# Layer 1's mixer gate summed by VectorE, block 0's products of chunk 1 in the passage, and a new list for the mixer

## The chip, the cores and the metric

One Trainium2 chip, one NeuronCore of it. The metric is the device time of one execution in microseconds (us). The engines are TensorE (PE in the profile; its weight loads are PEld), VectorE (DVE), ScalarE (ACT), GpSimd (POOL) and SyncE (SP), which issues all the loads of weights.

## The reference

Two layers work on x (256 tokens, 1024 features, f32) under a condition c (1024 values). Each has a mixer and an FFN:

```python
mod = silu(c) @ w_ada[l] + b_ada[l]
sh1, sc1, gt1, sh2, sc2, gt2 = split(mod, 6)
h = rms_norm(x, g_pre_mix) * (1 + sc1) + sh1
q, k, v, pz = split(h @ w_in[l])            # 4 x 512 columns
ao = causal_attention(rope(q), rope(k), v)  # 8 heads of 64
po = multiscale_pool(pz, w_pool, pool_scale)
y = concat(rms_norm(ao), rms_norm(po)) @ w_out[l]
x = x + gt1 * rms_norm(y, g_post_mix)
h = rms_norm(x, g_pre_ffn) * (1 + sc2) + sh2
u = causal_conv3(h @ w_up[l]) + conv_b      # 2 x 2816 columns
x = x + gt2 * rms_norm((silu(u_a) * u_g) @ w_down[l], g_post_ffn)
```

With 256 tokens there is one attention block, so the attention is plain causal softmax attention. gt1 is what this text calls the mixer gate.

## The kernel before

**Products in three parts.** Every f32 operand of a large product is split in two: a rounded part (hi for weights, hh for activations, sh for the FFN's gated activations) and the rest (lo, hl, sl). `mm3` does hi,hh, then lo,hh, then hi,hl, 512 columns each. ScalarE casts the hi, VectorE subtracts for the lo.

**The stream of weights.** `Stream` lists all weights as units of up to 128x2048 f32 in the order in which they are wanted. SyncE loads them in that order into four raw buffers (`RAW_BUFS`); a unit's load is issued when the unit four places ahead in the list is done with. `high` and `low` turn half units into parts (hi and lo, `PART_BUFS` = 8 of each); `ahead` makes parts up to six ahead of their use.

**Tokens and features.** Tokens stand in two blocks of 128. `Normed.trans` transposes the normed x (xn) on TensorE into tiles T, 128 features (a chunk, k or j from 0 to 7) by 256 tokens, and `Normed.make` scales and shifts a chunk into hh (ScalarE) and h, then hl (VectorE).

**Stages.** Layer 0's mixer; its FFN, 22 steps of an up product (u), the convolution and gate (`conv_glu`) and the down product (d), the last six down products kept to the end (`DEFER`); then the passage: the down products end for block 0 and block 1 (`tail`), two norms per block (ry for the FFN's output, rx for the new x), then layer 1's qkv stage, which goes over eight chunks and for each over two blocks; layer 1's mixer; layer 1's FFN.

**The modulation.** Most of mod comes from VectorE: `dot` multiplies a 128x1024 half unit with silu(c) on all partitions and sums each row (CUSTOM_DVE_ANT_0 in the trace, ISA in the instruction order), one column of 128 outputs at a time; scale, shift and the last gate come so. The mixer gate comes from TensorE: `ada_gt` multiplies silu(c) with 1 MB units of w_gt, in plain f32, into the bank gacc; ScalarE copies it (grow), `group_trans` transposes it (gT) and `group_cols` adds it up.

**What sets the order.** In the mixers an order written out by hand: `ORDER[l]` is a list of steps, and `hold` (or `held`) keeps the engines to the order in which the program states the instructions. Names: `ph` a quarter of the pz product of a block, `cq`, `ck`, `cK`, `cv`, `cz`, `cZ` copies out of PSUM, `ro` the rotary of a block, `kq` the transposes of q or k, `sc` scores, `mx`, `ex`, `rc`, `nm` softmax, `yP` and `wo` out products, `hi` and `lo` weight parts, `xu`, `xN`, `tr` the new x, its norm and its transposes, `wm` n dummy transposes. Everywhere else a scheduler orders each engine's instructions.

## Time and profile before

| | |
|---|---|
| three runs | 600.38, 602.14, 603.25 us; median 602.14 |
| the profiled execution | 601.36 us, of which 599.6 us from the first to the last instruction |
| mean granted TensorE clock | 0.998 |
| TensorE busy | 585.6 us |
| VectorE busy | 499.4 us |

Times in the rows count from the first instruction. TensorE's busy time counts a product from its issue to its modelled end, and products overlap, so what one costs is read from the distance of two starts. Idle time stands in brackets with the instruction that ended it.

### The profile page before, as it was taken

What the parts mean: (1) busy time and instruction counts of PE and PEld (TensorE: products, weight loads), DVE (VectorE), ACT (ScalarE), POOL (GpSimd) and SP (SyncE); (2) the same over time, 40 slices, a digit from 0 to 9 for tenths busy, and PEclk for the clock granted to TensorE, in tenths of its full rate; (3) what the DMA queues carried; (4) which work ended last, traced back from release to release, by engine and by line L of the source; (5) the groups of instructions that cost most, each with busy time, mean ns of one, the idle gap of its engine ahead of it and who ended that gap; (6) DMA issues with size and microseconds to landing.
All of it is one profiled execution on the core that took longest, in us unless ns stands there. A gap on an engine that the chain in (4) does not pass through costs nothing.

```text
span 599.6 us, 9775 instructions
## 1 busy us (share of the span) xinstructions
PE 585.6 (98%) x3783; PEld 508.8 (85%) x3783; DVE 499.4 (83%) x893; ACT 371.1 (62%) x659; POOL 25.7 (4%) x53
## 2 busy tenths in 40 slices
PE   8999999899999999999999999999999999999995
PEld 5787777699999999999858877789999999999984
DVE  6898899899999999999869675788989787777853
ACT  5557885875645565546547587888755565565641
POOL 1000012200000000000010001220000000000000
PEclk9999999999999999999999999999999999999999
DMA  8999878966898888988739832236576476545001
GB/s 330 415 383 392 332 301 314 359 228 220 346 342 318 320 315 291 350 315 316 279 105 362 331 145 72 74 137 232 199 275 238 179 260 232 192 167 205 1 0 70
DMA packets 22943, 149.08 MB, mean 249 GB/s; under 512 B 2801, under 2 KB 3313, under 8 KB 6642
## 3 DMA queue, kind: packets, MB, share of 16 engines
q1 hardware_dynamic: 22608, 148.37, 66.6%
q8 instruction: 29, 0.48, 0.3%
q10 hardware_dynamic: 290, 0.10, 0.1%
q14 instruction: 16, 0.13, 0.1%
HBM read 147.41 MB, written 1.05 MB: 248 GB/s over the span
## 4 chain that ended last, share of the span: by engine, by line
PE 80%; DVE 7%; DMA 4%; ACT 3%; issue 3%; POOL 1%; ACTq 0%; POOLq 0%; DVEq 0%; SPq 0%
PE u L69 39%; PE d L69 19%; PE qk L69 4%; PE yp L69 4%; DVE lo L69 3%; PE y L69 3%; PE pz L69 2%; PE v L69 2%; DMA raw<-w_a_d 2%; DVE raw L69 1%; DMA vecs<-vec_d 1%; DMA raw<-w_down_d 1%; PE sc L69 1%; ACT hi L69 1%; PE gacc L69 1%
## 5 line engine op out<-in xcount | busy, mean ns | idle before, releaser
L69 DVE TENSOR_TENSOR lo<-raw,hi 128x1024 fp32r<-128x1024 f32 (+1 forms) x182 | 215.2, 1197 | 19.3 <-ACT hi L69 19.0
L69 ACT CAST hi<-raw 128x1024 fp32r<-128x1024 f32 (+1 forms) x182 | 182.1, 1028 | 41.7 <-DMA raw<-w_up_d 15.3
L69 PE MATMUL u<-hh,hi 128*128 128x256 f32 x704 | 182.2, 282 | 0.0
L69 PE MATMUL u<-hh,lo 128*128 128x256 f32 x704 | 182.0, 282 | 0.0
L69 PE MATMUL u<-hl,hi 128*128 128x256 f32 x704 | 138.9, 282 | 0.9 <-DVE hl L69 0.9
L69 PEld LDWEIGHTS u<-hh,hi 128*128 128x128 f32 x704 | 132.6, 188 | 1.8 <-ACT hh L69 0.5
L69 PEld LDWEIGHTS u<-hh,lo 128*128 128x128 f32 x704 | 132.5, 188 | 1.4
L69 PEld LDWEIGHTS u<-hl,hi 128*128 128x128 f32 x704 | 107.2, 188 | 1.4 <-DVE hl L69 1.4
L69 DVE SCALAR_TENSOR_TENSOR cv<-u,vecs,cv 128x254 f32<-128x254 f32 (+1 forms) x176 | 82.7, 479 | 22.0 <-ACT cv L69 20.5
L69 DVE CUSTOM_DVE_ANT_0 raw<-raw,cbc,vecs 128x1024 f32<-128x1024 f32 x70 | 88.9, 1278 | 2.8 <-DMA raw<-w_a_d 1.4
L69 ACT ACTIVATE cv<-u,vecs 128x256 f32<-128x256 f32 x88 | 48.8, 558 | 59.2 <-PE u L69 59.2
L69 PE MATMUL d<-hi,sh 128*128 128x512 f32 x176 | 69.7, 396 | 0.3 <-ACT sh L69 0.3
L69 PE MATMUL d<-lo,sh 128*128 128x512 f32 x176 | 69.2, 393 | 0.0
L69 PE MATMUL d<-hi,sl 128*128 128x512 f32 x176 | 68.6, 394 | 0.0
L69 ACT CAST sh<-cv 128x256 fp32r<-128x256 f32 x44 | 17.6, 404 | 40.3 <-DVE cv L69 40.3
L69 PEld LDWEIGHTS d<-hi,sl 128*128 128x128 f32 x176 | 33.1, 188 | 7.8
L69 PEld LDWEIGHTS d<-hi,sh 128*128 128x128 f32 x176 | 33.1, 188 | 7.2 <-ACT sh L69 0.9
L69 PEld LDWEIGHTS d<-lo,sh 128*128 128x128 f32 x176 | 33.2, 189 | 6.2
L69 ACT ACTIVATE cv<-cv 128x256 f32<-128x256 f32 x44 | 18.4, 417 | 18.2 <-DVE cv L69 18.1
L69 DVE TENSOR_TENSOR sl<-cv,sh 128x256 fp32r<-128x256 f32 x44 | 18.4, 422 | 7.3 <-ACT sh L69 7.3
L69 PE MATMUL qk<-hi,hh 128*128 128x512 f32 x64 | 22.6, 403 | 0.7 <-ACT hh L69 0.7
L69 PE MATMUL qk<-lo,hh 128*128 128x512 f32 x64 | 22.8, 397 | 0.0
(148 smaller groups left out, 722.8 us busy)
## 6 DMA issues: line engine op xcount, KB each, us to landing
raw<-w_up_d SPq DMA_DIRECT2D x44, 1024.0 KB, 5.2
raw<-w_down_d SPq DMA_DIRECT2D x22, 1024.0 KB, 6.2
raw<-w_a_d SPq DMA_DIRECT2D x14, 1024.0 KB, 6.4
raw<-w_gt_d SPq DMA_DIRECT2D x12, 1024.0 KB, 4.8
raw<-w_out_d SPq DMA_DIRECT2D x8, 1024.0 KB, 7.8
raw<-w_s_d SPq DMA_DIRECT2D x8, 1024.0 KB, 6.9
raw<-w_g_d SPq DMA_DIRECT2D x8, 1024.0 KB, 5.2
raw<-w_qkv_d SPq DMA_DIRECT2D x8, 768.0 KB, 5.8
```

Of the source, the lines that this page charges most:

```text
L69: r = op(*a, **k)
```

## The change

**The mixer gate of layer 1.** Its four w_gt units, the 16 matmuls on them, the copies and the four transposes are gone. Four units w_g1 of two half units each take their place in the stream, and eight dots on VectorE sum them into mod: four between the chunks of the qkv stage, four as steps `s3` of the list. Of the four w_t2 units (parts of layer 1's second shift), whose eight dots all stood in layer 0's FFN, two stay there; one goes behind that FFN's last step (`LATE`) and one into the qkv stage.

**The passage.** `passage` replaces `tail` for layer 0 and states the order of all engines. The transposes and parts of block 0's chunks 0 and 1 stand among the last down products; behind these come block 0's products of chunk 0 and of chunk 1, then block 1's transposes.

**The mixer's list** is another: the eight `ph` steps stand at its start, and the last out products have another order. **The first two steps of layer 1's FFN** have a stated order: `ffn_in` does all hh,hi, then hh,lo, then hl,hi; `conv_in` does both convolutions.

```diff
+LATE = {NJ - 2: 2}
...
-    "gr cq0 pg cK0 cv0 ro0 cq1 ck1 ph00 cv1 ro1 ph10 hi6 hi7 lo6 kq01 kq00 tQ00 kq11 lo7 ph20 tQ01 tq11 sc0 "
...
-    "mh3 ml3 wo100 sa3 hi10 wo001 wo101 hi11 lo10 ss hi12 wo200 lo11 r1 wo201 hi13 gt0 lo12 yP12 r20 gg0 lo13 "
-    "yP13 r21 ad00 hi14 ad01 wo300 cy10 wo301 hi15 lo14 wo010 yG00 cy11 wo110 yq00 lo15 ey0 wo011 yq01 sy0 "
-    "ad10 gt1 ry0 ad11 gg1 wo210 xu00 wo310 yG01 xs00 wo111 eX0 xu01 yq10 wo211 ey1 yG10 xs01 wo311 sx0 yq11 "
-    "rx0 sy1 xN00 yG11 ry1 wm10 tr00 xu10 xu11 xs10 xN01 eX1 xS11 wm15 tr01 rx1 xN10 xN11 wm12 tr10 tr11",
...
+    "ph01 ph00 cv0 ph10 cv1 cq1 s320 cK1 ph20 tx s331 ph30 cq0 ck0 cZ0 ro1 ph11 hi6 pg ph21 hi7 ro0 ph31 kq01 "
+    "lo6 cZ1 kq00 lo7 kq10 tQ00 wi0 tQ10 s330 wi1 cd0 tq01 po0 cd1 sc1 sq5 s321 sq4 gm po1 mh4 mh5 mx10 sc0 "
+    "ml5 sq6 sa5 mh6 ml4 gt1 ex10 mx00 kq11 tq11 sa6 gg1 yP00 rc10 ex00 ml6 mx11 sc2 mh7 nm10 ex11 mx01 yP01 "
...
+    "wo101 hi12 wo200 lo11 hi13 r20 wo201 ad00 gt0 hi14 r21 ad01 gg0 wo300 ad10 wo301 yq00 ad11 ey0 wo210 "
+    "yq01 sy0 yG00 wo310 ry0 yG10 hi15 wo111 wo211 xu00 yq10 ey1 wo311 yG01 xs00 eX0 yq11 xu01 sy1 yG11 xs01 "
+    "ry1 sx0 xu10 rx0 xN00 xs10 xu11 eX1 wm25 tr00 xS11 xN01 rx1 wm11 tr01 xN10 xN11 tr10 tr11",
...
+                          + [(add_s2, 1, i) for i in range(4)] + [(add_t2, 1, i) for i in range(2)]):
...
             for k in range(1, NK):
                 st.add(w_qkv[k], 1536, [(0, 1024), (1024, 1536)])
+                if k in (3, 5):
+                    add_g1(k // 2 - 1)
+                if k == 5:
+                    add_t2(1, 3)
             for u in range(2):
                 st.add(w_pz[u], 2048, half2)
-            for u in range(4):
+            add_g1(2)
+            st.add(w_out[1, 2], 2048, half2)
+            add_g1(3)
+            for u in range(1, 4):
...
+            if l == 0 and i in LATE:
+                add_t2(1, LATE[i])
         if l == 0:
             st.add(w_qkv[0], 1536, [(0, 1024), (1024, 1536)])
-            for u in range(4):
-                add_gt(1, 0, u)
...
+    def w_block(nh, qk, v, k, b, n=0):
+        sl = slice(b * 128, (b + 1) * 128)
+        hh, hl = nh.h[k]
+        for i, o in enumerate(qk[b] + [v[b]]):
+            w = st.part(n + i // 2)
+            cs = slice(i % 2 * 512, i % 2 * 512 + 512)
+            mm3(o, hh[:, sl], hl[:, sl], w[0][:, cs], w[1][:, cs], start=(k == 0), stop=(k == NK - 1))
+    def passage(mms, ys, g):
+        yg = [w4("yg") for b in range(2)]
+        ry = [norm(lambda hf, b=b: ys[b][hf], "ry") for b in range(2)]
+        rx = [norm(lambda hf, b=b: xt[b][:, halves[hf]], "rx", True) for b in range(2)]
+        nh = Normed(1, False)
+        def gated(b, hf):
+            ve.tensor_mul(yg[b][:, halves[hf]], ys[b][hf], g[:, halves[hf]])
+        def update(b):
+            r = ry[b][1]()
+            for hf in range(2):
+                x = xt[b][:, halves[hf]]
+                ve.scalar_tensor_tensor(x, yg[b][:, halves[hf]], r, x, op0=OP.mult, op1=OP.add)
+                rx[b][0](hf)
+        def normed(b):
+            r, xn = rx[b][1](), w4(f"xn{b}")
+            for hf in range(2):
+                ve.tensor_scalar(xn[:, halves[hf]], xt[b][:, halves[hf]], r, None, op0=OP.mult)
+            return xn
+        for hf in range(2):
+            mms(0, hf)
+            ry[0][0](hf)
+            gated(0, hf)
+        update(0)
+        hold(True)
+        mms(1, 0)
+        ry[1][0](0)
+        xn = [normed(0)]
+        gated(1, 0)
+        mms(1, 1, 0, 1)
+        st.high()
+        st.low()
+        mms(1, 1, 1, 3)
+        for j in range(4):
+            nh.trans(j, 0, xn[0])
+        mms(1, 1, 3, DEFER)
+        nh.make(0, nh.src(0), False, 0)
+        st.high()
+        st.low()
+        nh.make(1, nh.src(1), False, 0)
+        ry[1][0](1)
+        gated(1, 1)
+        update(1)
+        xn.append(normed(1))
+        qk = [[bank("acc", f"qk{b}{i}") for i in range(2)] for b in range(2)]
+        v = [bank("ps", f"v{b}") for b in range(2)]
+        for k in range(2):
+            w_block(nh, qk, v, k, 0, 2 * k)
+        for j in range(4):
+            nh.trans(j, 1, xn[1])
+        for j in range(2):
+            nh.make(j, nh.src(j), False, 1)
+        for j in range(2, 4):
+            nh.make(j, nh.src(j), False)
+        hold(False)
+        return nh, qk, v, xn
...
+        def high(self, j):
+            a, s = self.ab(j)
+            self.h.append(act_parts("h"))
+            se.activation(self.h[j][0], self.src(j), AF.Identity, scale=a, bias=s)
+        def low(self, j):
+            a, s = self.ab(j)
+            th, tl = self.h[j]
+            h = wk.tile([128, S], F32, tag="h32", name="h32", bufs=2)
+            se.activation(h, self.src(j), AF.Identity, scale=a, bias=s)
+            ve.tensor_sub(tl, h, th.bitcast(F32))
...
-            def w_in_block(k, b):
-                wqk, wv = st.part(0), st.part(1)
-                w_in(qk[b], k, b, wqk, 0, 2)
-                w_in([vps[b]], k, b, wv, 0)
-            vps = [bank("ps", f"v{b}") for b in range(2)]
-            for b in range(2):
-                for j in range(4):
-                    nh.trans(j, b, xn[b])
-                nh.make(0, nh.src(0), False, b)
-                if b == 0:
-                    w_in_block(0, 0)
-            gap()
-            for j in range(1, 4):
-                nh.make(j, nh.src(j), False)
+            nh, qk, vps, xn = xn
             for k in range(NK):
-                for b in range(0 if k else 1, 2):
-                    w_in_block(k, b)
+                for b in range(0 if k > 1 else 1, 2):
+                    w_block(nh, qk, vps, k, b)
...
+                if 2 <= k < 6:
+                    n = k - 2
+                    dot(1, G1[n // 2], n % 2, 16 + n)
+                    if n % 2:
+                        st.free(G1[n // 2])
+                if k == NK - 2:
+                    dots(1, T2[1, 3], (30, 31))
...
+            if not l:
+                group_cols(l, 0, 16)
...
+        def s3(j, n):
+            dot(l, G1[j], n, 16 + 2 * j + n)
+            if n:
+                st.free(G1[j])
...
+    def ffn_in(nh):
+        us = [bank("ps", "u") for j in range(2)]
+        for k in range(NK):
+            nh.high(k)
+        for k in range(NK):
+            for j in range(2):
+                wh = st.parts[st.used + 2 * j + k // 4][0]
+                for i in range(2):
+                    up_k(us[j], nh, k, i, wh, 0, first=(k == 0 and i == 0))
+        for n in range(4):
+            if st.lows <= st.used + n:
+                st.low()
+            wl = st.parts[st.used + n][1]
+            for k in range(4 * (n % 2), 4 * (n % 2) + 4):
+                for i in range(2):
+                    up_k(us[n // 2], nh, k, i, wl, 0)
+        for k in range(NK):
+            nh.low(k)
+            if k in (3, 6):
+                st.ahead(5 + k // 6)
+            for j in range(2):
+                wh = st.parts[st.used + 2 * j + k // 4][0]
+                for i in range(2):
+                    up_k(us[j], nh, k, i, wh, 1, last=(k == NK - 1))
+        return us
...
+    def conv_in(l, us):
+        st.high()
+        st.high()
+        st.low()
+        ts = [w2("cv").rearrange("p (a s) -> p a s", a=2) for j in range(2)]
+        sl = [act_parts("s") for j in range(2)]
+        def taps(j, i):
+            ch = j + i * NJ
+            cw = [vecs[:, l, V_CW + n * 44 + ch:V_CW + n * 44 + ch + 1] for n in range(3)]
+            p, t = us[j][:, i * 256:(i + 1) * 256], ts[j]
+            se.activation(t[:, i], p, AF.Identity, scale=cw[2], bias=vecs[:, l, V_CB + ch:V_CB + ch + 1])
+            for n in (1, 0):
+                ve.scalar_tensor_tensor(t[:, i, 2 - n:], p[:, :S - 2 + n], cw[n], t[:, i, 2 - n:],
+                                        op0=OP.mult, op1=OP.add)
+        for i in range(2):
+            for j in range(2):
+                taps(j, i)
+        for j in range(2):
+            se.activation(ts[j][:, 0], ts[j][:, 0], AF.Silu)
+            ve.tensor_mul(ts[j][:, 0], ts[j][:, 0], ts[j][:, 1])
+            if not j:
+                st.low()
+        for j in range(2):
+            se.copy(sl[j][0], ts[j][:, 0])
+            ve.tensor_sub(sl[j][1], ts[j][:, 0], sl[j][0].bitcast(F32))
+        st.high()
+        st.low()
+        for i in range(4):
+            st.use()
+        return dict(enumerate(sl))
...
+            ve.held = j == NJ - 1
             ve.tensor_sub(sl, t[:, 0], sh.bitcast(F32))
+            ve.held = False
...
+                with behind(ve):
+                    pre_coef(1, True, 0, 8)
+                    dots(1, T2[1, 2], (28, 29))
...
-    def gap():
-        for u in range(4):
-            ada_gt(1, 0, u, "ps")
-    nh = mixer(1, xn, gap)
+        xn = ffn(0, nh, us, s)
     with behind(se, ve, te):
-        ffn(1, nh)
+        nh = mixer(1, xn)
+    hold(True)
+    us = ffn_in(nh)
+    s = conv_in(1, us)
+    hold(False)
+    with behind(se, ve, te):
+        ffn(1, nh, us, s)
```

How the instructions move. In the passage TensorE had, behind the last down product (d) of block 1, block 0's transposes, nine products of chunk 0 and the gate (gacc):

```order
L69 MATMUL d_1492<-hi,sl 128x512
L69 MATMUL T<-ident,xn_3327 128x128 x4
L69 MATMUL qk_3366<-hi,hh 128x512
L69 MATMUL qk_3366<-lo,hh 128x512
L69 MATMUL qk_3367<-hi,hh 128x512
L69 MATMUL qk_3367<-lo,hh 128x512
L69 MATMUL v_3370<-hi,hh 128x512
L69 MATMUL v_3370<-lo,hh 128x512
L69 MATMUL gacc<-raw,ctt 32x512 x5
L69 MATMUL qk_3366<-hi,hl 128x512
L69 MATMUL qk_3367<-hi,hl 128x512
L69 MATMUL v_3370<-hi,hl 128x512
```

Now it has there, behind the last down product, the nine products of chunk 0 (their last one is the first row) and those of chunk 1, and then block 1's transposes:

```order
L70 MATMUL v_3393<-hi,hl 128x512
L70 MATMUL qk_3389<-hi,hh 128x512
L70 MATMUL qk_3389<-lo,hh 128x512
L70 MATMUL qk_3389<-hi,hl 128x512
L70 MATMUL qk_3390<-hi,hh 128x512
L70 MATMUL qk_3390<-lo,hh 128x512
L70 MATMUL qk_3390<-hi,hl 128x512
L70 MATMUL v_3393<-hi,hh 128x512
L70 MATMUL v_3393<-lo,hh 128x512
L70 MATMUL v_3393<-hi,hl 128x512
L70 MATMUL T<-ident,xn_3386 128x128 x4
L70 MATMUL qk_3391<-hi,hh 128x512
```

Block 0's transposes have moved up between the down products, and no gate stands between block 0 and block 1.

VectorE in the qkv stage had, around the lo of chunks 5 to 7, only subtractions and the h of the later chunks:

```order
L69 TENSOR_TENSOR lo<-raw,hi 128x512
L69 TENSOR_TENSOR lo<-raw,hi 128x1024
L69 TENSOR_SCALAR h_3589<-T,coef_80,mod_78 128x256
L69 TENSOR_TENSOR lo<-raw,hi 128x512
L69 TENSOR_TENSOR hl<-h_3589,hh 128x256
L69 TENSOR_SCALAR h_3597<-T,coef_80,mod_78 128x256
L69 TENSOR_TENSOR hl<-h_3597,hh 128x256
L69 TENSOR_TENSOR lo<-raw,hi 128x1024 x6
```

Now four dots (ISA raw, the second row of each being the read of its sum) stand between h, hl and the lo of chunk 6, which is the last row:

```order
L70 ISA raw,mod_78<-raw,cbc,vecs 128x1024
L70 ISA mod_78 128x1
L70 TENSOR_TENSOR hl<-h_3548,hh 128x256
L70 TENSOR_SCALAR h_3556<-T,coef_80,mod_78 128x256
L70 ISA raw,mod_78<-raw,cbc,vecs 128x1024
L70 ISA mod_78 128x1
L70 TENSOR_TENSOR hl<-h_3556,hh 128x256
L70 ISA raw,mod_78<-raw,cbc,vecs 128x1024
L70 ISA mod_78 128x1
L70 ISA raw,mod_78<-raw,cbc,vecs 128x1024
L70 ISA mod_78 128x1
L70 TENSOR_TENSOR lo<-raw,hi 128x1024
```

The dots were not in this stage at all; two of them are on w_g1, two on w_t2.

At the end of layer 1's mixer VectorE had block 0's first half of xn (xn_4278) ahead of the two halves of block 1's new x (x_71, x2):

```order
L69 TENSOR_SCALAR xn_4278<-x_70,rx 128x512
L69 SCALAR_TENSOR_TENSOR yg<-y_4225,ra,gate 128x512
L69 SCALAR_TENSOR_TENSOR x_71<-yg,ry,x_71 128x512 x2
L69 TENSOR_SCALAR xn_4278<-x_70,rx 128x512
L69 ISA sqs,rx<-x_71,rx 128x512
L69 ISA rx 128x1
L69 TENSOR_SCALAR xn_4331<-x_71,rx 128x512 x2
```

Now that half of xn (xn_4252) stands between them:

```order
L70 SCALAR_TENSOR_TENSOR yg<-y_4137,ra,gate 128x512
L70 SCALAR_TENSOR_TENSOR x_71<-yg,ry,x_71 128x512
L70 TENSOR_SCALAR xn_4252<-x_70,rx 128x512
L70 SCALAR_TENSOR_TENSOR x_71<-yg,ry,x_71 128x512
L70 ISA sqs,rx<-x_71,rx 128x512
L70 ISA rx 128x1
L70 TENSOR_SCALAR xn_4252<-x_70,rx 128x512
L70 TENSOR_SCALAR xn_4313<-x_71,rx 128x512 x2
```

Block 1's second half of x, and with it the square sum behind it, has come behind block 0's first half of xn.

## Rows read from the trace of the kernel before

**Rows 1.** The page's first part: TensorE, busy us, share of the span, instructions.

```profile
PE 585.6 (98%) x3783; PEld 508.8 (85%) x3783; DVE 499.4 (83%) x893; ACT 371.1 (62%) x659; POOL 25.7 (4%) x53
```

**Rows 2.** TensorE's timeline in the passage: start us, us, instructions, [idle before <-releaser].

```profile
304.13 0.60 PE L69 MATMUL T<-ident,xn 128*128 128x128 f32 x4
...
307.00 1.90 PE L69 MATMUL gacc<-raw,ctt 128*32 128x512 f32 x10
...
309.99 0.66 PE L69 MATMUL T<-ident,xn 128*128 128x128 f32 x4
...
310.57 2.77 PE L69 MATMUL gacc<-raw,ctt 128*32 128x512 f32 x22
...
313.28 0.50 PE L69 MATMUL qk<-hi,hh 128*128 128x512 f32 x1
```

**Rows 3.** ScalarE's timeline in the passage.

```profile
304.92 0.45 ACT L69 ACTIVATE hh<-T,mod,coef 128x128 fp32r<-128x128 f32 x1
...
305.26 0.29 ACT L69 ACTIVATE ry<-msy,ry 128x1 f32<-128x1 f32 x1
...
310.46 0.46 ACT L69 ACTIVATE hh<-T,mod,coef 128x128 fp32r<-128x128 f32 x1 [2.74 <-PE T L69]
```

**Rows 4.** TensorE's timeline near the last step of layer 0's FFN.

```profile
289.65 0.39 PE L69 MATMUL d<-hi,sh 128*128 128x512 f32 x1
289.88 0.40 PE L69 MATMUL d<-lo,sh 128*128 128x512 f32 x1
290.54 0.50 PE L69 MATMUL d<-hi,sh 128*128 128x512 f32 x1 [0.26 <-ACT sh L69]
```

**Rows 5.** VectorE's timeline at the same place.

```profile
290.36 1.27 DVE L69 CUSTOM_DVE_ANT_0 raw<-raw,cbc,vecs 128x1024 f32<-128x1024 f32 x1
291.56 0.08 DVE L69 DVE_READ_ACCUMULATOR2_ANT mod<- 128x1 f32 x1
```

**Rows 6.** TensorE's timeline in layer 1's mixer.

```profile
360.93 0.60 PE L69 MATMUL gT<-ident,grow 128*128 128x128 f32 x4
361.36 2.04 PE L69 MATMUL pw<-tab,pz 128*128 128x144 f32 x16
```

**Rows 7.** Stages: length, busy PE PEld DVE ACT POOL, granted clock, DMA share, GB/s.

```profile
313.30:343.50 30.20, 30.20 (x137) 24.38 (x135) 23.25 (x32) 20.24 (x28) 0.00 (x0) 1.00 0.94 347
343.50:397.10 53.60, 53.60 (x303) 42.06 (x302) 39.69 (x110) 42.65 (x102) 7.51 (x11) 1.00 0.35 127
397.10:404.20 7.10, 6.57 (x55) 5.68 (x53) 5.28 (x10) 5.46 (x12) 1.92 (x4) 1.00 0.00 1
```

**Rows 8.** VectorE's groups by form, whole run: busy us, mean ns, idle before.

```profile
L69 DVE TENSOR_TENSOR lo<-raw,hi 128x1024 fp32r<-128x1024 f32 x174 | 210.3, 1221 | 19.3 <-ACT hi L69 19.0
...
L69 DVE TENSOR_TENSOR hl<-h,hh 128x256 fp32r<-128x256 f32 x31 | 12.5, 420 | 1.6 <-ACT h L69 1.5
...
L69 DVE TENSOR_TENSOR lo<-raw,hi 128x512 fp32r<-128x512 f32 x8 | 5.5, 684 | 0.0
...
L69 DVE TENSOR_SCALAR h<-T,coef,mod 128x256 f32<-128x256 f32 x7 | 3.7, 541 | 1.7 <-ACT hh L69 1.7
```

**Rows 9.** DMA issues from 280 to 410 us: KB each, median us to landing.

```profile
raw<-w_qkv_d SPq DMA_DIRECT2D x8, 768.0 KB, 5.8
...
raw<-w_gt_d SPq DMA_DIRECT2D x4, 1024.0 KB, 4.8
```

**Rows 10.** TensorE's timeline at the end of layer 1's mixer.

```profile
397.14 1.25 PE L69 MATMUL wm<-ident 128*128 128x128 f32 x10
...
404.18 0.39 PE L69 MATMUL u<-hh,hi 128*128 128x256 f32 x1
...
405.13 0.28 PE L69 MATMUL u<-hh,lo 128*128 128x256 f32 x1
...
406.09 0.75 PE L69 MATMUL u<-hl,hi 128*128 128x256 f32 x4 [0.68 <-DVE hl L69]
```

**Rows 11.** VectorE's timeline at the same place.

```profile
398.18 0.49 DVE L69 TENSOR_SCALAR xn<-x,rx 128x512 f32<-128x512 f32 x1 [1.11 <-POOL rx L69]
```

More of the change, by code (lines that the diff above doesn't have):

```diff
@@ L237, in add_t2, with add_g1 @@
         T2[l, j] = st.add(w_t2[j], 2048)
+    def add_g1(j):
+        G1[j] = st.add(w_g1[j], 2048)
     def add_g2(l, j):
@@ L965, in steps, with up_k @@
         return nh
-    def ffn(l, nh):
-        acc, s = None, {}
+    def up_k(u, nh, k, i, w, low, first=False, last=False):
+        cs = slice((k % 4) * 256 + i * 128, (k % 4) * 256 + (i + 1) * 128)
+        te.matmul(u[:, i * 256:(i + 1) * 256], w[:, cs], nh.h[k][low], start=first, stop=last,
+                  skip_group_check=True)
+    def ffn_in(nh):
[23 more added lines that the diff above has]
+        return us
```

86 lines of the change are left out of this document (47 added, 39 removed), and 9 rows, old and new, of the table ORDER.

## The prediction

> **What bounds the kernel now.** I read the page's first part, then the timelines of TensorE and ScalarE in the passage from layer 0 to layer 1, those of TensorE and VectorE at the end of layer 0's FFN, the busy time by stage, VectorE's groups by form, the DMA issues, and last the end of layer 1's mixer. The page shows TensorE busy in 585.6 of 599.6 us [rows 1]. So only two things can pay: work taken off TensorE, and the few stretches in which it waits. Consecutive 512-column products start 0.23 us apart (289.65, 289.88) [rows 4]; I use 0.2325, the mean of long runs of them.
>
> The passage is the one place where layer 1 loses much. The down projection ends at 304.13; the first product of chunk 0 with block 1 starts at 313.28 [rows 2]: 9.15 us. In them TensorE does nine products of block 0 (9 x 0.2325 = 2.09), eight transposes (about 0.5 for four) and 32 records of the mixer gate (10 from 307.00, 22 from 310.57) [rows 2]. In the stages after it (313.3 to 343.5 and 343.5 to 397.1) it is busy 30.20 of 30.20 and 53.60 of 53.60 us [rows 7]: nothing can be won there except by removing work, and every new wait is a loss.
>
> **The passage: 4.8 won, 0.5 given back.** The gate records go. What then sets block 1's first product is the chain from the last down product through block 1's two norms. Before, its transposes start at 309.99, 5.86 us after 304.13 [rows 2]. In that chain ScalarE does an hh cast (start 304.92) ahead of the 128x1 step that yields ry (start 305.26) [rows 3]; in the stated order that cast is done among the down products, so the chain is 0.34 shorter: 5.5. Then from the transposes to the end of hh: 310.46 + 0.46 - 309.99 = 0.93 [rows 2, 3]. So block 1's first product starts 6.45 us after the last down product, where it was 9.15: 2.70 won. In the meantime TensorE does 18 products of block 0 (chunks 0 and 1), 4.19 us, nine more than before: 2.09 won, 4.8 together. It still idles, about 1.3 us before block 1's transposes and 0.5 behind them: the gate had hidden that chain, which is what is late next. Block 0's four transposes now stand among the down products and lengthen these by 0.5. Bounds: 0.34 less, if the cast was no hindrance, and 0.3 more.
>
> **The gate's end: 0.43 won.** The four transposes gT, 360.93 to 361.36 [rows 6], and VectorE's adds on them are gone. ScalarE's copies of grow stood beside TensorE's products, so their going gains nothing.
>
> **The last step of layer 0's FFN: 0.2 won.** Before, TensorE loses 0.66 - 0.23 = 0.43 us at 289.88, for sh [rows 4]; VectorE runs a dot just then [rows 5]. In the changed kernel two dots are gone from there to the mixer, and two stand behind the last sl. But its TensorE also asks for the last sh some 2.6 us sooner, about where I count it to be ready. Bounds -0.5 and +0.43; I take 0.2. A dot costs 1.20 from its start to the next (290.36 to 291.56) [rows 5]. The two behind sl end before the first yg can start; without that cover they would delay block 0's norm, which the down products of block 1 hide.
>
> **The qkv stage: 0.9 lost.** Here the gate comes back as VectorE's work: eight dots of w_g1 and two of w_t2 enter layer 1's mixer. Six of them (four of w_g1, two of w_t2) stand among the lo subtractions of the chunks. VectorE is busy 23.25 of 30.20 us there [rows 7]; six dots add 7.2, and chunk 1's two lo, now made in the passage, take away 1.9 (1.22 and 0.68) [rows 8]: 28.5. The stage is 2.1 us shorter, since chunk 1's block 0 is done: 28.1. VectorE is full. Who pays is decided by its order: four dots stand directly ahead of chunk 6's lo. Start to start an instruction costs some 0.08 less than its mean, as the dot's 1.20 against 1.27 shows [rows 5]. Counted from the last down product: the first hh of block 1 at 6.45, its h and hl and those of chunks 1 to 3 until about 10.2, six dots 7.2, four lo pairs 7.0, four h and hl 3.2 (0.46 and 0.34 each), chunk 6's first lo 1.14 [rows 8]: 28.7. TensorE wants that lo at 6.45 + 2 x 2.09 + 4 x 4.19 + 1.0 (transposes and restarts) = 28.4. A late load adds up to 1.3 in VectorE's queue (chunk 5 waits for chunk 2's slot). So 0.3 to 1.6; I take 0.9. Bounds 0 and 4.8 (all four dots on the path). The Trainium skill, page Perfetto Trace Analysis, section Identifying the Most-Contended Engine, holds occupancy to be a fair measure of VectorE's headroom; by it 77% busy before leaves room for the dots, and the sum below would be 5.3. I don't follow it: a queue in order can be late for one chunk with room left over the stage.
>
> **The mixer's new list: nothing, up to 2 lost.** VectorE is busy 39.69 of 53.60 us from 343.5 [rows 7]; four more dots make 44.5. The list puts all 48 pz products (48 x 0.2325 = 11.2 us) right behind the chunks, and VectorE's backlog (two dots, the key copy, both rotaries) hides behind them. In my count it ends 1 to 2 us before TensorE asks for it at the key transposes; if it doesn't, the scores are late next.
>
> **The end of the mixer: 0.4 lost.** From the last out product (397.14) to the first up product (404.18) TensorE has only transposes, for 7.04 us [rows 10]; block 1's norm sets the end. Before, VectorE makes block 0's first xn at 398.18 [rows 11], ahead of block 1's two x updates. Block 0's last out products now stand three groups of products, 2.1 us, closer to the end, and the listed order puts that xn between block 1's two updates. It waits for block 0's power, which I put 3.2 us after the last product, where 1.04 were enough before; then come the second update, the square sum, the power and the last xn. I get 7.4 in place of 7.04. Bounds 7.0 and 8.2. The dummy transposes are 36 instead of 37 and cost nothing, because TensorE waits there anyway.
>
> **The first up products: 0.8 won.** Before, TensorE loses 406.09 - 405.13 = 0.96 us, less a product of 0.12, waiting for the first hl [rows 10]. In the stated order the 32 products hh,hi and the 32 hh,lo come first, 7.7 us in which the four lo and the first hl are made. What is late next is the gated activation for the first down product, behind which the third unit's up products stand as cover. Everything outside these places keeps its instructions, and the w_g1 loads have the bytes of the w_gt loads.
>
> **Sum.** 4.8 - 0.5 + 0.4 + 0.2 - 0.9 - 0.4 + 0.8 = 4.4 us won. The profiled run took 601.36 us (span 599.6), 0.78 below the median of 602.14. 4.4 less is 597.0 from the one and 597.7 from the other; I predict 597.3.
>
> **Rivals.** *VectorE becomes the bound in layer 1 (0.23).* The dots cost 3.6 us more of TensorE's time than I allow, at chunk 6, at the pz products or at the key transposes: 0.8 won, about 601.3. For it: VectorE needs 28.5 of 28.1 us, in order. Against it: 11.2 us of pz products as a buffer.
>
> *Slower (0.09): loads that wait for dots.* The loads are issued in order into four raw slots. The load of w_t2 takes the slot of w_g1's first unit and so waits for the second dot on it; chunks 6 and 7 and pz stand behind. A chunk took 5.8 us to land [rows 9], then come a cast and a lo. In my count chunk 6 lands 2.6 us before VectorE asks for it. If loads come 4 to 5 us later than counted, TensorE waits some 2 us at chunks 6 and 7 and at both pz units: 8 lost, 602.1 - 4.4 + 8 = 605.7. The point is a landing over 2.6 us late. Against it: a gate unit of 1 MB landed in 4.8 us [rows 9], and chunks 1 to 3 are now loaded ahead of the passage.
>
> *The clock (0.03).* The two idle stretches in the passage are longer than those seen here. The granted clock was 1.00, the 2.4 GHz level, in all three stages shown, even from 397.1 to 404.2, where TensorE ran transposes alone [rows 7]. If it fell to 1.2 GHz in the passage, block 1's 18 products of chunks 0 and 1 would take 0.2325 more each: 4.2 lost, about 602. The Trainium skill, page TensorE: Matmul & The Clock Gate, section PE-mode transpose, says that transposes don't count as busy for the clock as products do; by that rule the end of the mixer would run at the low level, before as after, and the trace doesn't agree.
>
> *More than counted (0.05).* Chunk 6 never waits, the end of the mixer takes 7.0, the last FFN step gains its 0.43 and the passage idles 0.6 less: 4.4 + 0.9 + 0.4 + 0.2 + 0.6 = 6.5 won or more, below 595.6.
>
> **Numbers.** Runs of this kernel spread from 600.4 to 603.3, so 0.5% (3.0 us) is about what a measurement tells from no change. My forecast, 2 to 6.5 us won, has 0.60, of which 0.55 lies beyond 3.0. With the last rival, faster by over 0.5% has 0.60. Slower has 0.09. Within 0.5% has the rest, 0.31: 0.05 of the forecast, VectorE as the bound, and the clock. The range leaves out the slower case and the far end of the last one: 594.8 to 601.6.
>
> **What would show it.** The passage: no gacc, 18 block-0 products behind the last down product, 1 to 1.5 us idle before block 1's transposes, and block 1's first product 6.2 to 6.8 us after the last down product. The qkv stage: one wait of TensorE for lo at chunk 6, under 2 us, and VectorE without idle. Behind it no wait at the key transposes. The end of the mixer: 7.0 to 8.2 us, and no wait for hl behind it. The prediction is wrong if TensorE's waits in layer 1's mixer pass 3 us together, if the loads named above come late, or if the passage's chain is longer than 6.8.

## The result and the profile after

The changed kernel takes 598.09 us (median; 596.98 to 598.66), 0.9944 of the kernel before (95% interval 0.9922 to 0.9966). I had forecast 597.3. Its profiled execution took 596.98 us with a span of 595.2, where before it was 601.36 and 599.6: 4.4 us less by the spans, 4.05 by the medians. With more executions of both kernels, on the chip of run 11 below, it is 3.0 us by the medians (600.83 and 597.81).

The page's first part, of the changed kernel:

```profile
span 595.2 us, 9693 instructions
PE 579.2 (97%) x3746; PEld 506.3 (85%) x3746; DVE 508.2 (85%) x912; ACT 368.4 (62%) x654; POOL 27.1 (5%) x53
```

TensorE is busy 6.4 us less [rows 1], and the span is 4.4 shorter: its idle time has grown by 2.0 us. Stage by stage, from the starts of TensorE's first and last instructions of each stage in the two timelines:

| stage | before | after | won | forecast |
|---|---|---|---|---|
| up to layer 0's first up product | 115.23 | 114.84 | 0.39 | 0 |
| layer 0's FFN, to the end of its down products | 188.90 | 189.09 | -0.19 | -0.3 |
| passage and qkv stage, to the first pz product | 41.56 | 37.24 | 4.32 | 3.9 |
| from there to the last out product of the mixer | 51.45 | 51.97 | -0.52 | 0.4 |
| end of the mixer, to the first up product | 7.04 | 7.80 | -0.76 | -0.4 |
| layer 1's FFN, to its last down product | 188.60 | 187.31 | 1.29 | 0.8 |
| behind that | 6.82 | 6.95 | -0.13 | 0 |

The first row is no effect of the change: the same stage took 114.38 to 115.45 in the kernels below.

**The passage.** TensorE's timeline, from the last down product to block 1's first products (columns: start and time in us; in brackets the idle time before, and what ended it); it answers to [rows 2]:

```profile
303.70 0.39 PE L70 MATMUL d<-hi,sl 128*128 128x512 f32 x1
303.93 0.39 PE L70 MATMUL qk<-hi,hh 128*128 128x512 f32 x1
...
307.87 0.39 PE L70 MATMUL v<-hi,hl 128*128 128x512 f32 x1
309.64 0.66 PE L70 MATMUL T<-ident,xn 128*128 128x128 f32 x4 [1.38 <-DVE xn L70]
310.63 0.50 PE L70 MATMUL qk<-hi,hh 128*128 128x512 f32 x1 [0.33 <-ACT hh L70]
```

TensorE does eighteen products of block 0 and no gate, and then loses 1.54 us (309.64 less 307.87, less 0.23) until VectorE's xn is there. Block 1's first product starts 310.63 - 303.93 = 6.70 us behind the end of the down products. ScalarE's timeline of the same place, against [rows 3]:

```profile
303.71 0.46 ACT L70 ACTIVATE hh<-T,mod,coef 128x128 fp32r<-128x128 f32 x1 [0.92 <-DVE h L70]
304.13 0.60 ACT L70 ACTIVATE sqs<-d 128x512 f32<-128x512 f32 x1
304.62 0.19 ACT L70 ACTIVATION_READ_ACCUMULATOR sqs<-d 128x1 f32 x1
304.91 0.29 ACT L70 ACTIVATE ry<-msy,ry 128x1 f32<-128x1 f32 x1
```

The step that yields ry starts 0.98 us behind the end of the down products; before it was 305.26 - 304.13 = 1.13. So only 0.15 of the 0.34 was won. ScalarE's two rows ahead of the cast, before:

```profile
304.33 0.60 ACT L69 ACTIVATE sqs<-d 128x512 f32<-128x512 f32 x1 [1.72 <-PE d L69]
304.83 0.19 ACT L69 ACTIVATION_READ_ACCUMULATOR sqs<-d 128x1 f32 x1
```

The square sum (sqs) starts 0.20 us behind the down products' end in both kernels, so chunk 1's hh, which now stands ahead of it, costs nothing. From the read of the sum to ry it was 0.43 us with the cast between them (304.83 to 305.26) and is 0.29 without it (304.62 to 304.91). That difference is what the cast cost.

**The qkv stage.** VectorE's timeline at chunk 6, the last of the dots and the first two lo behind it:

```profile
331.16 1.28 DVE L70 CUSTOM_DVE_ANT_0 raw<-raw,cbc,vecs 128x1024 f32<-128x1024 f32 x1
332.36 0.08 DVE L70 DVE_READ_ACCUMULATOR2_ANT mod<- 128x1 f32 x1
332.36 1.82 DVE L70 TENSOR_TENSOR lo<-raw,hi 128x1024 fp32r<-128x1024 f32 x2
```

And TensorE's timeline there, from chunk 5's last product:

```profile
332.42 0.40 PE L70 MATMUL v<-hi,hl 128*128 128x512 f32 x1
332.65 0.64 PE L70 MATMUL qk<-hi,hh 128*128 128x512 f32 x2
333.13 0.39 PE L70 MATMUL v<-hi,hh 128*128 128x512 f32 x1
333.36 0.40 PE L70 MATMUL qk<-hi,hh 128*128 128x512 f32 x1
333.64 0.50 PE L70 MATMUL qk<-lo,hh 128*128 128x512 f32 x1
```

The stages' busy time (columns as in [rows 7]): the qkv stage, the mixer, the mixer's end.

```profile
310.60:341.20 30.60, 30.57 (x135) 24.51 (x136) 28.17 (x44) 16.53 (x23) 0.00 (x0) 1.00 0.71 263
341.20:393.10 51.90, 50.93 (x289) 40.11 (x288) 39.88 (x114) 42.88 (x99) 6.11 (x10) 1.00 0.46 175
393.10:400.90 7.80, 6.47 (x53) 5.55 (x51) 6.43 (x12) 3.57 (x12) 2.90 (x6) 1.00 0.00 0
```

VectorE is as full as forecast: 28.17 us of 30.60, and the lo of chunk 6 starts behind the dots, 28.4 us after the down products' end. But TensorE first does four hi,hh products of the chunk (332.65 to 333.36) and asks for the lo only then, 0.99 us after the chunk's start. It loses 333.64 - 333.36 - 0.23 = 0.05 us.

**The mixer.** At the key transposes, where I had forecast no wait, TensorE's timeline shows one:

```profile
352.10 0.40 PE L70 MATMUL pz<-hi,hl 128*128 128x512 f32 x1
353.40 1.50 PE L70 MATMUL qT<-ident,qk 128*128 128x128 f32 x12 [0.90 <-DVE qk L70]
```

That is 1.07 us beyond a product. VectorE's timeline ahead of it, to the end of the rotary:

```profile
345.16 2.36 DVE L70 TENSOR_TENSOR lo<-raw,hi 128x1024 fp32r<-128x1024 f32 x2 [3.16 <-ACT hi L70]
347.44 1.28 DVE L70 CUSTOM_DVE_ANT_0 raw<-raw,cbc,vecs 128x1024 f32<-128x1024 f32 x1
348.64 0.08 DVE L70 DVE_READ_ACCUMULATOR2_ANT mod<- 128x1 f32 x1
348.64 1.28 DVE L70 CUSTOM_DVE_ANT_0 raw<-raw,cbc,vecs 128x1024 f32<-128x1024 f32 x1
349.85 0.09 DVE L70 DVE_READ_ACCUMULATOR2_ANT mod<- 128x1 f32 x1
349.85 0.69 DVE L70 COPY qk<-qk 128x512 f32<-128x512 f32 x1
...
352.83 0.42 DVE L70 TENSOR_TENSOR qk<-qk,rope 128x256 f32<-128x256 f32 x1
```

And ScalarE's, which makes the hi of the same unit:

```profile
344.08 2.00 ACT L70 CAST hi<-raw 128x1024 fp32r<-128x1024 f32 x2 [3.53 <-DMA raw<-w_out_d]
345.99 1.06 ACT L70 COPY v<-v 128x512 f32<-128x512 f32 x2
```

Both engines stand still for over 3 us on a load of w_out (issued at 335.95, cast from 344.08), whose parts nothing needs yet; two dots and the rotary are queued behind it. The length of the wait differs from one execution to the next: in the five later profiles whose list is the same up to this place (runs 2, 4, 7, 8 and 11) it is 0.29 to 1.74 us.

**The end of the mixer.** VectorE's timeline, against [rows 11]:

```profile
395.23 0.75 DVE L70 SCALAR_TENSOR_TENSOR x<-yg,ry,x 128x512 f32<-128x512 f32 x1 [0.26 <-POOL ry L70]
396.42 0.49 DVE L70 TENSOR_SCALAR xn<-x,rx 128x512 f32<-128x512 f32 x1 [0.44 <-POOL rx L70]
396.82 0.75 DVE L70 SCALAR_TENSOR_TENSOR x<-yg,ry,x 128x512 f32<-128x512 f32 x1
```

Block 0's xn waits for its power between block 1's two updates, as forecast. Behind it the first up products have no wait (400.94, 404.84, 408.64 are the starts of the three runs of 32), where [rows 10] showed 0.96 us from one product to the next.

### The profile page after: what moved, and what is told of

It reads as the page before. It is cut to its first block, busy times and chain, and to the rows that moved or that the text cites. A ratio compares the mean times of both kernels' runs of the same rounds, so it can differ in the third digit from the quotient of the medians.

```text
span 595.2 us, 9693 instructions
## 1 busy us (share of the span) xinstructions
PE 579.2 (97%) x3746; PEld 506.3 (85%) x3746; DVE 508.2 (85%) x912; ACT 368.4 (62%) x654; POOL 27.1 (5%) x53
## 3 DMA queue, kind: packets, MB, share of 16 engines
HBM read 147.41 MB, written 1.05 MB: 249 GB/s over the span
## 4 chain that ended last, share of the span: by engine, by line
PE 76%; DVE 10%; DMA 5%; issue 3%; ACT 3%; POOL 1%; ACTq 0%; POOLq 0%; DVEq 0%; SPq 0%
PE u L70 42%; PE d L70 19%; PE yp L70 4%; DVE lo L70 4%; PE y L70 3%; DVE raw L70 3%; DMA raw<-w_a_d 2%; DMA raw<-w_out_d 1%; DMA raw<-w_g_d 1%; PE sc L70 1%; ACT sqs L70 1%; DMA vecs<-vec_d 1%; PE ao L70 1%; ACT hi L70 1%; PE pT L70 1%
## 5 line engine op out<-in xcount | busy, mean ns | idle before, releaser
L70 PE MATMUL u<-hh,hi 128*128 128x256 f32 x704 | 178.2, 282 | 0.0
L70 PE MATMUL u<-hh,lo 128*128 128x256 f32 x704 | 178.0, 282 | 0.0
L70 PE MATMUL u<-hl,hi 128*128 128x256 f32 x704 | 137.5, 282 | 0.3 <-DVE hl L70 0.3
L70 PEld LDWEIGHTS u<-hh,hi 128*128 128x128 f32 x704 | 130.4, 188 | 2.0 <-ACT hh L70 0.5
L70 PEld LDWEIGHTS u<-hh,lo 128*128 128x128 f32 x704 | 130.3, 188 | 1.4
L70 DVE CUSTOM_DVE_ANT_0 raw<-raw,cbc,vecs 128x1024 f32<-128x1024 f32 x78 | 98.8, 1276 | 2.0 <-DMA raw<-w_a_d 1.4
```

The source lines that it names most:

```text
L70: r = op(*a, **k)
```

## The experiments

Each is an edit of the changed kernel; the numbers are in the order of running, and 7 and 8 stand beside 4, which they split. Times are medians, with the ratio to the kernel before from the same chip and its 95% interval; the stage times are of one profiled execution of each kernel. The kernel before took 600.7 to 600.8 in these runs, where its first measurement gave 602.14.

**1. The first out unit's parts behind the rotary.**

```diff
-                st.ahead()
+                st.ahead(LEAD if k < NK - 1 else 4)
-ro1 ph11 hi6 pg ph21 hi7 ro0 ph31 kq01 lo6 cZ1 kq00 lo7 kq10
+ro1 ph11 hi4 pg ph21 hi5 ro0 ph31 kq01 lo4 hi6 lo5 cZ1 hi7 kq00 lo6 lo7 kq10
```

> The two hi and lo parts of the first out unit of layer 1 are no longer made in the qkv stage but behind the rotary of block 0; nothing else moves. Theory A (VectorE's queue is held by those two lo, whose load lands late; the dots and the rotary stand behind them): the wait of TensorE ahead of the key transposes, 1.07 us in the changed kernel, is gone, VectorE's rotary ends before the last pz product, and the span falls by about 1.0 us (595.2 to 594.2; median 598.1 to 597.1). Theory B (VectorE has simply too much work from chunk 6 on, whatever the order): the rotary ends as late as before, the wait stays, span within 0.3 us of 595.2.

598.40 us, 0.9967 [0.9954, 0.9979]. The wait at the keys is gone (48 pz products in 11.20 us), but the time is not: pz to the last out product takes 52.47. TensorE's timeline shows where it went:

```profile
355.40 1.07 PE L70 MATMUL po<-pd,wpool 128*128 128x256 f32 x4
357.80 0.93 PE L70 MATMUL sc<-k,q 64*128 64x128 f32 x8 [1.33 <-DVE k L70]
```

The scores now wait for VectorE's key copy, which stands behind the two lo that were moved, two others and a dot. Theory A holds for the place of the wait, not for the gain.

**2. Block 0's xn behind both updates of block 1.**

```diff
-xu10 rx0 xN00 xs10 xu11 eX1 wm25 tr00 xS11 xN01 rx1 wm11 tr01 xN10 xN11 tr10 tr11
+xu10 rx0 xs10 xu11 eX1 xS11 xN00 rx1 xN01 wm36 tr00 tr01 xN10 xN11 tr10 tr11
```

> At the end of layer 1's mixer block 0's first half of xn stands behind both x updates and the square sum of block 1, and the 36 dummy transposes stand ahead of all transposes. Theory A (VectorE's second update of block 1 waits for block 0's power, as the prediction had it): last out product to first up product goes from 7.80 to about 6.8, span 594.2, median 597.1. Theory B (block 1's own chain, its power and squares on ScalarE and GpSimd, sets the end, and the order on VectorE doesn't matter): 7.8 stays, within 0.2. If block 0's transposes, now later, become what is late, 7.3 to 7.6.

597.78 us, 0.9948 [0.9930, 0.9966]; span 594.2. The end of the mixer takes 7.16 in place of 7.80: theory A, with 0.64 of the 1.0. The runs can't tell this kernel from the changed one. Block 0's transposes wait for their xn, and all sixteen follow in one piece:

```profile
398.07 1.96 PE L70 MATMUL T<-ident,xn 128*128 128x128 f32 x16 [1.11 <-DVE xn L70]
```

**3. Only chunk 0 in the passage.**

```diff
-        for k in range(2):
+        for k in range(1):
             w_block(nh, qk, v, k, 0, 2 * k)
-                for b in range(0 if k > 1 else 1, 2):
+                for b in range(0 if k else 1, 2):
```

> The passage does only chunk 0 with block 0; chunk 1's nine products of block 0 go back behind block 1's first products. Theory A (block 1's norm chain sets its first product, and the products of chunk 1 only fill TensorE's wait): the first product of block 1 stays 6.7 us behind the last down product, TensorE idles 3.6 instead of 1.5 us, and the span grows by 2.1 us less what the later chunks' lo parts then have as room, so 596.9 to 597.3; median 599.8 to 600.2. Theory B (the qkv stage is set by VectorE at chunk 6, so what the passage gains is given back there): span within 0.4 of 595.2. Theory C (the products compete with the chain): block 1's first product comes earlier than 6.5 us, and the span grows by less than 1.5.

599.04 us, 0.9975 [0.9965, 0.9986]. Block 1's transposes start 5.72 us behind the down products (5.71 in the changed kernel): theory A, the chain is as long without chunk 1's products on TensorE. The loss in passage and qkv stage is 40.06 - 37.24 = 2.82, not 2.1, for a reason that none of the theories had. After 3.46 us of idle TensorE's granted clock is 0.55, most of the stretch at the lower of its two levels (columns as above):

```profile
311.90:315.60 3.70, 3.69 (x12) 3.01 (x13) 2.64 (x7) 1.93 (x5) 0.00 (x0) 0.55 0.00 0
315.60:320.00 4.40, 4.40 (x20) 3.58 (x19) 4.32 (x7) 4.40 (x7) 0.00 (x0) 0.99 0.00 0
```

At that level products start 0.42 to 0.43 us apart. So chunk 1's products fill 2.1 us, and by filling them they keep the idle at 1.4 us, behind which the clock fell in one of ten profiles (run 11). The medians are only 0.95 to 1.2 us apart (598.09 and 597.81 for the changed kernel): the profiled execution of this run is its slowest (600.85). The mixer takes 50.84 where it was 51.97, with no wait at the keys; that VectorE and the loads catch up in the longer qkv stage fits this, and is not shown by itself. This profiled execution also has a wait of 1.8 us at 281.81, in layer 0's FFN, for VectorE's cv.

**4. The first up products unstated, their lo back in the list.** The kernel before had it so.

```diff
-    us = ffn_in(nh)
-    s = conv_in(1, us)
+    us, s = None, {}
-hi13 r20 ... gg0 wo300 ad10 ... hi15 wo111 wo211
+hi13 lo12 r20 ... gg0 lo13 wo300 ad10 ... hi15 lo14 wo111 lo15 wo211
```

> The first two up steps of layer 1's FFN are left to the scheduler, as in the kernel before, and the last four lo parts of the mixer go back into its list; the rest is as changed. Theory A (the stated order hides the wait for the first hl): the wait of about 0.8 us at the first hl product is back, and the span grows by 0.8 to 1.2 us (596.0 to 596.4; median 598.9 to 599.3). Theory B (the FFN of layer 1 is shorter for another reason): no growth beyond 0.3. The lo parts in the list may lengthen the end of the mixer, by up to 0.5.

603.14 us, 1.0040 [1.0028, 1.0051]: slower than before the change, and further from the changed kernel than either theory. The mixer takes 2.0 more (53.99), its end 11.79. Layer 1's FFN is only 0.27 longer (187.58): the wait for hl is not back. The end of the mixer is 4.0 longer, time in which VectorE can make the lo and hl. Runs 7 and 8 split this edit.

**7. Only the four lo back in the list.**

> Of the kernel with unstated first up products only one part: the four lo parts of the first up units go back into the mixer's list, where the kernel before had them; the order of the up products stays as changed. Theory A (the 6 us that the earlier run lost come from these four lo, 4.6 us of VectorE in front of block 1's norm, and from the clock behind the longer idle): span 600.8 to 601.5, last out product to first up product 11 to 12 us, granted clock near 0.5 in it. Theory B (they come from the order of the up products): span within 0.5 of 595.2.

602.08 us, 1.0018 [1.0008, 1.0029]; span 600.9. Theory A: the mixer takes 54.27, its end 10.97. The transposes stand behind 3.27 us of idle and run at a lower clock:

```profile
395.78:401.90 6.12, 2.90 (x26) 2.65 (x24) 5.37 (x9) 3.31 (x10) 2.27 (x5) 1.00 0.49 174
401.95:406.75 4.80, 4.80 (x27) 4.56 (x27) 2.55 (x6) 0.61 (x2) 0.73 (x1) 0.64 0.00 0
```

**8. Only the order of the up products undone, the four lo kept behind the last xn.**

> The other part alone: the order of the first up products is left to the scheduler, the four lo parts stay behind the mixer's last xn on VectorE. Theory A (the stated order hides the lo and hl behind the first 64 products): TensorE waits for lo and hl early in the first up products, 0.8 to 3 us, and the end of the mixer stays 7.8; span 596.0 to 598.0. Theory B (the order of the products is worth nothing): span within 0.3 of 595.2.

603.38 us, 1.0048 [1.0029, 1.0068]; span 600.9. The mixer and its end stay (52.13, 7.80); layer 1's FFN takes 193.00 where it was 187.31. TensorE waits for lo and hl in the first products, and then its granted clock falls, with no idle stretch over 1.1 us in layer 1 so far:

```profile
403.74 0.39 PE L70 MATMUL u<-hh,lo 128*128 128x256 f32 x1 [0.95 <-DVE lo L70]
405.21 1.22 PE L70 MATMUL u<-hl,hi 128*128 128x256 f32 x4 [0.85 <-DVE hl L70]
```

```profile
404.30:411.20 6.90, 6.05 (x29) 5.99 (x29) 6.90 (x13) 6.01 (x12) 0.00 (x0) 0.51 0.88 347
```

In that stretch 28 products take 6.05 us (405.21 to 411.26), where at the usual 0.12 us they take 3.4: an estimate of 2.7 us for the clock. The nine products ahead of them lose some 3.1 to waits, just over what I had put (0.8 to 3). So theory A holds in kind, and the rest of the 5.7 us is the clock; how much of it TensorE would have waited for VectorE at the full clock, since VectorE was busy in all of that stretch, stays open. The order of the products and the late lo belong together: either alone makes the kernel slower than it was before.

**5. No dots in layer 1's mixer.** The same is done with the other dots there.

```diff
+    def touch(i, n, ch):
+        ve.tensor_copy(mod[1][:, ch:ch + 1], st.raw(i)[:, n * D:n * D + 1])
...
-                    dot(1, G1[n // 2], n % 2, 16 + n)
+                    touch(G1[n // 2], n % 2, 16 + n)
```

> The ten dots of layer 1's mixer (eight of the gate, two of w_t2) are left out: each becomes a 128x1 copy out of the loaded unit, so that all loads and their order stay, and the output is not the reference's. Theory A (VectorE is just full: the qkv stage is not slowed by the dots, and the mixer behind it is, at the key transposes and the scores): last down product to first pz product stays 37.2 us within 0.3, pz to last out product falls from 51.97 to about 50.8 with no wait ahead of the key transposes, span about 594.0, median 1.2 under the changed kernel's. Theory B (VectorE bounds all of layer 1's first part): also the qkv stage falls, by 1 us or more, span below 593. Theory C (late loads set the wait at the key transposes, not the dots): the wait of 1 us stays, span within 0.4 of 595.2.

596.32 us, 0.9928 [0.9913, 0.9943]; span 594.4. Theory A, in this profile: the qkv stage is not shorter (37.54), the mixer is 1.1 us shorter (50.89), with no wait at the keys (48 pz products in 11.20 us). The size is less sure than that: profiles of kernels with the changed list took 51.17 to 52.13 in the mixer (the changed kernel, runs 2, 8 and 11), and the interval of this run overlaps the changed kernel's. VectorE's pause for the load of w_out is still there (3.30 us), and costs nothing now.

**6. Six products of chunk 2 more in the passage.** The two new calls do block 0's hi,hh and hi,hl; ScalarE casts chunk 2 between block 1's two norms (those lines are left out here).

```diff
+        third(nh, qk, v, 4, 0, 0)
+        third(nh, qk, v, 4, 0, 1)
         for j in range(4):
             nh.trans(j, 1, xn[1])
...
```

> Six of block 0's nine products of chunk 2 (hi with hh and hi with hl) are done in the passage, between chunk 1's products and block 1's transposes; ScalarE casts chunk 2 there, and its lo products stay in the qkv stage. Theory A (TensorE's 1.5 us ahead of block 1's transposes are free time, set by block 1's norm chain): block 1's transposes still start 5.7 to 5.9 us behind the last down product, pz starts 35.9 to 36.3 behind it where it was 37.24, and the span falls by 0.9 to 1.4 us where VectorE's chunk 6 lo keeps up. Theory B (VectorE is already just on time at chunk 6, so work that TensorE does sooner is waited for there): pz stays at 37.0 to 37.3, span within 0.4 of 595.2. Theory C (the added casts and h lengthen the chain): transposes at 6.3 or later, span 595.8 or more.

599.10 us, 0.9976 [0.9962, 0.9991], 1.0 us over the changed kernel's first median, with intervals that overlap a little. Passage and qkv stage are 0.73 shorter (36.51; transposes at 6.01), but more than that is lost at the keys, where TensorE loses 2.80 us:

```profile
355.14 1.07 PE L70 MATMUL qT<-ident,qk 128*128 128x128 f32 x8 [2.63 <-DVE qk L70]
```

None of the three theories had this place. VectorE idles 3.35 us for the same late unit, and the lo of it start 1.0 us later than in the changed kernel, counted from the down products (42.25 and 41.23).

**9. As 1, with the key copy ahead of the lo too.**

```diff
-ro0 ph31 kq01 lo6 cZ1 kq00 lo7 ... cd0 tq01
+ro0 ph31 kq01 tq01 lo4 cZ1 lo5 hi6 kq00 hi7 lo6 kq10 tQ00 wi0 lo7 ... cd0
```

> As the first experiment (the hi and lo of layer 1's first out unit are made behind the rotary), and now the key copy of VectorE stands ahead of those lo too. Theory A (rotary and key copy wait in order behind the hi and lo of a unit that lands late; moving that whole chain ahead of them takes the wait away, and the four lo have room behind it, since the out products ask for them later): no wait at the key transposes, none over 0.6 us at the scores, pz to last out product 50.9 to 51.3 where it was 51.97, span about 594.3. Theory B (VectorE's work is simply too much; the wait comes back further on, at the softmax or the out products): pz to last out product 51.8 to 52.5, span 595 to 595.7.

600.14 us, 0.9993 [0.9982, 1.0004]. The key copy is in time, TensorE idles 0.84 us for ScalarE's pd, and the long wait stands at the softmax, where four lo and two dots are ahead of it on VectorE:

```profile
362.56 0.65 PE L70 MATMUL gps<-ident,coef 128*128 128x128 f32 x4 [1.85 <-DVE st L70]
```

It is theory B by the place, and larger: pz to the last out product takes 53.91, where B had at most 52.5.

**10. Edits 2, 6 and 9 together.**

> Three edits together: the key chain ahead of the late unit's hi and lo, block 0's xn behind both updates of block 1 at the mixer's end, and six of block 0's products of chunk 2 in the passage. If they add: passage and qkv stage 36.5 behind the last down product (37.24), pz to last out product 51.0 to 51.5 (51.97), end of the mixer 7.16 (7.80), span about 593.0, 2.2 under the changed kernel's. If what TensorE wins in the passage is only waited for in the mixer (loads and VectorE set its pace): mixer 52.2 or more, span 594 to 594.5.

599.47 us, 0.9977 [0.9965, 0.9990]. Passage and qkv stage take 35.81, the end 7.17, and the mixer between them 56.22: they don't add. VectorE now waits 3.30 us for the load of a w_g1 unit ahead of the rotary. TensorE idles 2.64 us at the softmax, and behind that its clock is at the lower level:

```profile
362.86 0.65 PE L70 MATMUL gps<-ident,coef 128*128 128x128 f32 x4 [2.64 <-DVE st L70]
```

```profile
364.10:367.60 3.50, 3.50 (x14) 2.05 (x12) 3.40 (x20) 3.09 (x11) 0.00 (x0) 0.51 0.99 410
```

**11. The changed kernel again.**

> The changed kernel itself, for a comparison on the same chip: 0.9944 of the kernel before within the interval, pz to last out product 51.5 to 52.0, wait ahead of the key transposes 0.6 to 1.1 us.

597.81 us, 0.9951 [0.9935, 0.9967], and a profiled execution of 597.3 us span that shows what varies. After the same idle as before (1.36 us) products run 0.42 us apart for some 3 us:

```profile
311.30 0.66 PE L70 MATMUL T<-ident,xn 128*128 128x128 f32 x4 [1.36 <-DVE xn L70]
...
314.69 0.63 PE L70 MATMUL v<-hi,hh 128*128 128x512 f32 x1
315.11 0.63 PE L70 MATMUL v<-lo,hh 128*128 128x512 f32 x1
315.54 0.63 PE L70 MATMUL v<-hi,hl 128*128 128x512 f32 x1
```

The granted clock of 312.29 to 317.29 is 0.66; passage and qkv stage take 38.55, the mixer 51.17, and TensorE loses only 0.29 us at the keys. The ratio is as expected; both the mixer and that wait lie below what I had put (51.5 to 52.0, 0.6 to 1.1). Layer 0's FFN is 1.05 us longer (190.14), with 0.97 us lost at 281.96 for VectorE's cv.

**12. Half of the gate late.** Edits 2 and 9, and the last w_g1 unit loaded behind the out units, its two dots where VectorE idled 4.2 us (before 381.57).

```diff
-            add_g1(3)
-            for u in range(1, 4):
+            for u in range(4):
                 st.add(w_out[1, u ^ 2], 2048, half2)
+            add_g1(3)
-cy10 at3 sq2 mh2 sa2 wo000 sq3 sa3 mh3 wo100 cy11 ml2 ml3 wo011 hi10
+cy10 at3 s330 s331 gm sq2 mh2 sa2 wo000 sq3 sa3 mh3 wo100 gt1 cy11 ml2 ml3 wo011 gg1 hi10
```

> The key chain stands ahead of the late unit's hi and lo as in the ninth run, block 0's xn behind both updates as in the second, and of the gate the two dots of the last w_g1 unit move from the start of the mixer to the place where VectorE idled 4.2 us behind the softmax (378 in the changed kernel); that unit is loaded behind the out units, and the gate's second row is made there too. Theory A (the waits at keys and scores come from the dots standing where VectorE and the loads are late, not from their number): no wait over 0.3 us at the key transposes and scores, pz to last out product 50.9 to 51.3 (51.97), end of the mixer 7.16 (7.80), span 593.4 to 594.2, median 1 to 1.8 under the changed kernel's. Theory B (they only move the wait: the dots then hold up the square sums and the gate's rows, or the four lo the softmax): pz to last out product 51.8 or more, span 594.5 or more.

598.56 us, 0.9958 [0.9945, 0.9971]. No wait at the keys and none over 0.3 us at the scores, but 0.84 us for ScalarE's pd ahead of the pool's products and 0.98 for VectorE's y among the last out products: 52.88 in place of 51.97. It is theory B: the wait has moved, once to ScalarE, which casts the parts, and once to VectorE.

## Why the prediction was right, and where it was not

**The passage: right.** With the 0.9 of the qkv stage the forecast was 3.9 won, measured are 4.32. The transposes come at 5.71 (forecast 5.5), the first product at 6.70 (6.45), the idle is 1.54 and 0.33 (1.3 and 0.5). Run 3 shows the mechanism: with nine products fewer the chain is as long. The term was 0.25 too large: 0.19 of it is the hh cast, which had cost 0.15 and not the 0.34 between two starts that I took, and the rest lies behind the transposes (0.99, forecast 0.93).

**The last step of layer 0's FFN: not settled.** The wait for sh (0.43) is not there in the profile after; in runs 3, 10 and 11 a wait of 1.0 to 1.8 for VectorE's cv stands some 8 us earlier. With the transposes among the down products (0.75, forecast 0.5) the stage lost 0.19, forecast 0.3.

**The qkv stage: the wrong place.** I forecast 0.9 lost at chunk 6's lo. VectorE was as late as forecast (its lo is done 29.65 us after the down products; 28.7 and up to 1.3 were counted), but TensorE asks for it 1.3 us later than my 28.4: the chunk starts at 28.72, and its first four products need no lo. I had not read that order. In run 5, without the dots, the stage is not shorter.

**The mixer's new list: failed.** "Nothing" was 1.07 lost at the key transposes, the place that I named for the case that the backlog is too long. The step that failed is the count by which VectorE ends 1 to 2 us ahead. It ends 0.9 behind: the backlog as I listed it lacks the two lo of the first out unit and the 3.16 us that VectorE idles for their load. Both are needed for the wait: without the dots it is gone (run 5), and with the dots, but without those two lo ahead of them, it is gone too (run 1). Its size is 0.29 to 1.74 us over the profiles. That another order of the same work would be free of it is not shown: runs 1, 9 and 12 each took the wait away from its place, and found it at the scores, the softmax, ScalarE or the out products. The 44.5 us of VectorE's work were wrong too, 39.88 measured; the four lo that leave the list, some 4.6 us, were not taken off.

The rule of the Trainium skill (Perfetto Trace Analysis, Identifying the Most-Contended Engine) that I weighed held for the qkv stage, where an occupancy of 92% (28.17 of 30.60) left TensorE with a wait of 0.05. It did not for the mixer, where 77% (39.88 us of 51.90) go with one of 1.07: by it this term would have stayed 0.

**The end of the mixer: right in kind, small.** 0.4 forecast, 0.76 measured, and run 2 gets 0.64 back by taking block 0's xn from between block 1's two updates, the step that I named.

**The first up products: right for the difference, and too small a view.** 0.84 of the 1.29 is the wait for hl that I named; where the other 0.45 comes from stays open. But I costed the stated order as if the rest of the list were given. Runs 7 and 8 show that four lo, 4.6 us of VectorE, had to leave the mixer for its new work to fit, and that they could leave without a loss only with this order. Without the pair the change would have been a loss (run 4: 1.0040). My rival of VectorE as the bound in layer 1 names the key transposes, where the wait came; its 3.6 us did not come.

**The total** came out near in part by luck, since errors cancel. By the table the change won 0.42 more than forecast in passage and qkv stage, 0.49 in layer 1's FFN and 0.11 in layer 0's, and 0.92 less in the mixer and 0.36 less at its end. Of the 4.4 us between the two spans 0.39 is the first row, which the change doesn't touch. And 3.0 us, the difference with more executions (run 11), is further from 4.4 than 4.05 is.

**The clock** fell in one of ten profiles of a passage with these eighteen products (run 11). That cost some 1.3 us, 38.55 less 37.24, and not the 4.2 of my rival: in this profile it was low for some 3 us, and there a product took 0.19 us more. It fell elsewhere too, in runs 3, 4, 7, 8 and 10, where the edit made TensorE wait. A profile is one execution, and others of the same kernel differ: the mean granted clock of an execution was 0.996 to 0.998 in the changed kernel, but 0.994 in nine of the eleven executions of run 9 (0.997 in the profiled one) and 0.992 to 0.999 in run 6 (0.999 in the profiled one). So part of what the medians of such runs lose is the clock, and their profiles don't show where.

No kernel here that computes the reference is shown to be faster than the changed one; run 2 has a shorter end of the mixer in its profile, and its runs don't tell it apart.

## What to carry to other kernels

Work that goes from the bound engine to one that has room needs room at its place in the queue, not in the mean: look for what stands behind it there, above all behind a load that is late. Where an edit moves two things (an order, and parts made later), undo them one at a time: here each alone cost 4.0 and 5.3 us by the medians, and together they paid for the move. And a wait that is taken away counts only when the stage has become shorter; runs 1, 9 and 12 only moved it on. A stage time of one profile is one execution: the mixer of the changed kernel took 51.97 us in one and 51.17 in another, so a difference of 1 us in one profile needs a second profile of the unchanged kernel.
